# Keeping four weight splits and two gated chunks on chip, moving the residual's loads to GpSimd's queue, and issuing short convolutions behind the next copies

## The chip, the core and the metric

The kernel runs on one core of one Trainium2 chip. The metric is the device time of one execution, in microseconds (us); the time before is the median of three runs. The engines go by the profile's names: PE is TensorE (matmuls), DVE is VectorE, ACT is ScalarE, POOL is GpSimd, SP is SyncE, which here does nothing but issue transfers. POOL and ACT issue transfers too, in the order of their own instructions.

## What is computed

One block of a streaming encoder on a sequence of 1024 tokens with 1024 channels, all in float32:

```python
h = rms_norm(x, norm_mix_g) * (1 + sc1) + sh1
b_s, c_s, v_s, v_c, gl_c, gate_br = split(h @ w_in)          # 7 x 1024 columns
y_a = (b_s * causal_dwconv(c_s * v_s, width 3)) @ w_short_out
u = causal_dwconv(v_c * sigmoid(gl_c), width 31) + conv_conf_b
y_b = silu(layer_norm(u)) @ w_conf_out
g_a, g_b = split(sigmoid(gate_br))
x = x + g1 * ((g_a * y_a + g_b * y_b) @ w_o)
h2 = rms_norm(x, norm_ffn_g) * (1 + sc2) + sh2
a, bgate = split(h2 @ w_ffn_in)                              # 2 x 2816 columns
x = x + g2 * ((silu(a) * bgate) @ w_ffn_out)
return rms_norm(x, final_norm_g)
```

The six vectors sh1, sc1, g1, sh2, sc2, g2 are the modulation, silu(c) @ w_ada + b_ada.

## The kernel before

**Layout and arithmetic.** Channels lie on the 128 partitions, in eight chunks, and the 1024 tokens on the free axis, in two halves of 512. A float32 product is made of three matmuls: each operand is split into a high part (a cast by ACT) and a low part (a subtraction by DVE or POOL), and `mm3` (L315) adds wh·xh, wh·xl and wl·xh (its lines L323, L324 and L326) into one bank of PSUM. Nearly every matmul is 128x128 by 128x512.

**Duals.** Most projections are done two column chunks at a time with seven products in place of eight ("dual"): sums and differences of blocks of the weights, and of blocks of the activations, are multiplied in the order `PRODUCTS = "1265734"`, and each product adds into one of three pairs of banks, x (1, 6, 7, 4), y (2) or z (5, 3). After product "1" ACT copies x to y, and "2" goes on adding there.

**Order of the work.** The kernel is written in the Tile language, which sets the semaphores and decides each engine's order of instructions when it compiles, by the order of the text and by when it reckons things ready. `tc.issue_after(ins)` puts the instructions of a block behind `ins` in the order of the same engine; it makes nobody wait. Weights come from a `plan`: `next_w` (L287) hands out the next unit and sees that the two that follow are begun. A plain unit (`weights`, L211) is a load on SP's queue into one of the raw buffers, a cast (L220) into one of three wh buffers and a subtraction (L221) into one of three wl buffers. Most activations and their splits live in one pool, `t`, of 58 tiles of 128x512.

The stages, with the lines that the change and the prediction's steps touch:

1. *Input projection.* Seven column chunks by plain products, then 14 duals (`win_dual`, L713; dual 0 to 5 have products "1" and "2" done ahead, so their loop begins with "6"). `PAIRS` (L76) says what each dual makes: "u" a channel chunk of the conformer, "p" one of the short convolution, "q" the multiplier of two short-conv chunks, "g" gates. The banks rotate by one pair from dual to dual, so the x banks of one dual are the z banks of the next. At the end of a dual, each "p" has its width-3 convolution done by `short_conv` (L667), which uses the x banks of its dual as room: one ACT activation (L671) and two DVE taps (L674) for each half. Meanwhile DVE does the width-31 convolution, tap by tap (L821), between the evictions. The copy from x to y is L769.
2. *Short-conv projection* `ya`, four column chunks at a time in two duals (L926).
3. *Conformer projection* `yb` (L994), for each half of the tokens in turn: eight weights w_conf[k], eight banks, three matmuls for each pair; the last two weights are done together at the end. The plan lists the eight weights twice, once for each half (L284). `next_b` (L898) makes the operands: a product with the layer norm's scale, silu, split (zs). The banks are evicted by DVE with the gate (L1002) and joined with y_a (L990, then the split into mg).
4. *Output projection* `mix` (L1013). The new residual x1 goes to DRAM (x1_dram), by POOL's queue.
5. *FFN in* (L1105 on): 11 duals, each a pair of gated chunks. `hid_set` (L1168) makes what the next stage multiplies. For the first nine pairs these are seven blocks for seven products; the last two pairs (chunks 18, 19 and 20, 21) are kept as they are, four halves each. `store` (L1161) splits each block into a stage buffer (three of them, 128x1024; ACT L363, DVE L364) and POOL's queue stores it to DRAM (L1166).
6. *FFN out* (L1268 on): three groups of three pairs, in each two duals ("column duals": chunks 0 to 3 with 4 to 7, here called dual 0 and 1 of the group), products of 18 matmuls each. `group_load` (L1197) loads a group's 42 tiles back from DRAM by POOL's queue (L1192) into pool t, the first group during the last dual of stage 5, each next one after the first product of the group before. `out_evac` (L1258) adds each bank onto x1 in place (DVE L1263): products "1", "2", "6" and "3" onto chunks 0 and 1 (dual 1: 2 and 3), "5", "7" and "4" onto 4 and 5 (dual 1: 6 and 7).
7. *Last chunks* 18 to 21 and the final norm, in three pieces of tokens (`piece_out`, L1305).

x1 comes back from DRAM before stage 6: chunks 0 and 1 by POOL's queue (L1251), into a pool of their own; the other six by SP's queue (L1256), in the order 4, 5, 2, 3, 6, 7, into a pool `x1b` that lies where stage 5's pools `gi` (the gated chunks) and `stage` lay.

Of the kernel before, what the change touches and what calls it, by code (L numbers as in the profile page):

```python
# [39 lines left out]
P = 128  # L40
D = 1024
T = 1024
H = 512
KC = D // P
# [55 lines left out]


FRONT = 3


GROUP, GROUPS = 3, 3
# [10 lines left out]
def block_kernel(ctx: ExitStack, tc: tile.TileContext, xt, x0, xT, c, vecs, ada, w_first, w_duals,  # L116
# [164 lines left out]
    ya_units = [dual_units([w_short[d, m] for m in range(4)], 1024, True, lo={"1": nc.vector if d else nc.gpsimd})  # L281
                for d in range(2)]
    plan += [ya_units[d][m] for d, m in ya_order]
    plan += [(w[k], 1024) for w in (w_conf, w_o) for _ in range(2) for k in range(KC)]  # L284
    ready = []

    def next_w(ahead=AHEAD):  # L287
# [141 lines left out]
    x = {}  # L429
# [268 lines left out]
    def q_operands(m):  # L698

        for k in range(KH):  # L700
# [9 lines left out]
                nc.vector.tensor_tensor(b12, b22, b12, ALU.subtract)  # L710
            tq[m][k] = split({"1": b11, "2": b21, "5": b11, "7": b12, "3": b22, "4": b21}[m], hl_tile, "tq")

    def win_dual(d, pairs, x, y, z):  # L713

        mul = any(kind == "q" for kind, *_ in pairs)

        def c11(p, e, kind, j, *more):
            if kind == "q":
                times(sc[j][:, halves[0]], y[p], sc[j][:, halves[0]])
                return  # L720
            first_out(d, p, y[p])

        def c22(p, e, kind, j, *more):
            src = y[p] if kind == "q" else e["5"]
            add = nc.vector.tensor_tensor(src, x[p], e["5"], ALU.add)
            if kind == "q":
                return minus_times(sc[j + 1][:, halves[1]], src, sc[j + 1][:, halves[1]])
            e["z"] = src
            if kind == "g":
                gate_out(more[0], 1, src, src, -1.0)  # L730
            elif kind == "u":
                nc.scalar.activation(src, src, AF.Sigmoid, scale=-1.0)
            return add

        def c12(p, e, kind, j, *more):
            add = nc.vector.tensor_tensor(z[p], z[p], e["6"], ALU.add)
            if kind == "q":
                return times(sc[j][:, halves[1]], z[p], sc[j][:, halves[1]])
            if kind == "u":
                return times(e["b"][1], z[p], e["z"])  # L740
            if kind == "p":
                return minus_times(e["b"][1], z[p], e["z"])
            gate_out(j, 1, z[p], e["6"])
            return add

        def c21(p, e, kind, j, *more):
            if kind == "q":
                return minus_times(sc[j + 1][:, halves[0]], x[p], sc[j + 1][:, halves[0]])
            if kind == "p":
                return minus_times(e["b"][0], x[p], e["b"][0])  # L750
            if kind == "u":
                nc.scalar.activation(x[p], x[p], AF.Sigmoid, scale=-1.0)
                return times(e["b"][0], x[p], e["b"][0])
            gate_out(more[0], 0, x[p], g_tile("sig"), -1.0)

        banks = {"1": x, "6": x, "7": x, "4": x, "2": y, "5": z, "3": z}
        at = 5 * d - 2 if d < AHEAD_DUALS else 7 * d - 2 * AHEAD_DUALS
        if d < AHEAD_DUALS:
            for p in range(2):
                nc.scalar.copy(x[p], m1[d, p])  # L760
        for m in PRODUCTS[2 if d < AHEAD_DUALS else 0 :]:
            w = next_w()
            for p in range(2):
                ps, e = banks[m][p], st[d][p]
                for k in range(KH):
                    c0 = (p * KH + k) * P
                    mm3([ps], slice(c0, c0 + P), w, [th[m][k]], m in "15" and k == 0, k == KH - 1, m not in "15")
                if m == "1":
                    nc.scalar.copy(y[p], ps)  # L769
                elif m in "65":  # L770
                    e[m] = g_tile("v")
                    nc.scalar.copy(e[m], ps)
                else:
                    done = {"2": c11, "7": c22, "3": c12, "4": c21}[m](p, e, *pairs[p])
                    if done is not None:
                        reads.append((at + AT_READS[m] + 0.5 * p, done.ins))
            if m == "6" and d < AHEAD_DUALS - 1:
                m1_load(d + 1)
            if m == "5" and MOD_FROM <= d < MOD_FROM + MOD_DUALS:
                modulation(16 + d - MOD_FROM, uc_tile("ada", D))  # L780
            if d == len(PAIRS) // 2 - 1:
                if m == "1":
                    for j in range(KH):
                        q_load(j)
                if m in "16734":
                    q_operands({"1": "1", "6": "2", "7": "6", "3": "5", "4": "7"}[m])
        for e, (kind, j, *more) in zip(st[d], pairs):
            if kind == "p":
                short_conv(j, e["t"], x)
            elif kind == "q" and j < KH:  # L790
                for i in range(2):
                    q_store(j + i)
# [363 lines left out]
                ha[f, "4"] = t  # L1156
        return evac

    hid_dram = {}

    def store(key, src):  # L1161

        s = stagep.tile([P, T], F32R, tag="stage", name="stage")
        t_split(src, s[:, :H], s[:, H:])
        hid_dram[key] = dram.tile([P, T], F32R, name="hid" + "_".join(map(str, key)))
        nc.gpsimd.dma_start(hid_dram[key], s)  # L1166

    def hid_set(d):  # L1168

        (b11, b12), (b21, b22) = ((ha[2 * d + p, "4"], ha[2 * d + p, "6"]) for p in range(2))  # L1170
        if 2 * d >= REST:
            for p, half in enumerate(((b11, b12), (b21, b22))):
                for h in range(2):
                    store((2 * d + p, h), half[h])
            return
        store((d, "1"), b11)
        store((d, "2"), b21)
        t2 = gip.tile([P, H], F32, tag="g", name="t2")
        nc.vector.tensor_tensor(b11, b11, b12, ALU.subtract)
        minus(t2, b11, b22)  # L1180
        store((d, "6"), t2)
        store((d, "5"), b11)
        nc.vector.tensor_tensor(b12, b22, b12, ALU.subtract)
        store((d, "7"), b12)
        store((d, "3"), b22)
        minus(b21, t2, b21)
        store((d, "4"), b21)
# [64 lines left out]
    close(*phase_2)  # L1252
    x1bp = open_pool("x1b", 6, stack=ctx)[1]
    x1 += [x1bp.tile([P, T], F32, tag="x1", name=f"x1{j}") for j in range(2, KC)]
    for j in (4, 5, 2, 3, 6, 7):
        nc.sync.dma_start(x1[j], x1_dram[j])  # L1256

    def out_evac(d):  # L1258
        def evac(p, m, ps):
# [5 lines left out]
            )  # L1265
        return evac

    hid = {}  # L1268
    n = 2 * GROUP * P
    for g in range(GROUPS):  # L1270
        for d in range(2):
# [2 lines left out]
    for g in range(GROUPS):  # L1274
        for d in range(2):
            banks = {}
            for m in PRODUCTS:
                product(banks, m, to[g, m], out_evac(d))
                if d == 0 and m == "1":
                    if g < GROUPS - 1:  # L1280
                        for q in PRODUCTS:
                            group_load(g + 1, q)
                    else:
                        for h in range(2):
                            for f in range(REST, FC):
                                hid[f, h] = t_load((f, h))


# [164 lines left out]
```

## Time and profile before

| | |
|---|---|
| median of three runs | 1468.57 us (1468.46 to 1469.9) |
| the profiled execution: its own time, its span | 1469.82 us, 1468.0 us |
| PE busy | 1447.8 us, 6393 matmuls |
| DVE busy | 1167.9 us, 1604 instructions |
| ACT busy | 652.7 us, 959 instructions |
| POOL busy | 527.4 us, 466 instructions |
| bytes read from and written to DRAM | 198.90 MB, 62.91 MB |
| mean granted TensorE clock | 0.996 |

The span is the time from the first instruction to the last of one execution that the hardware profiler recorded; that execution's own time is a little longer. A row of the timeline has its start in us from the span's start, its duration, engine, line, operation, the tiles (out<-in), the shapes, and in brackets how long the engine stood idle ahead of it and what ended that. A row of the waits has who waited for whom, then the total in us, how many times, and the longest. A row of the chain of waits has its start, how long, and what. A row of the windows has the stretch, its length, the busy time and (x) count of PE, PE's weight loads, DVE, ACT and POOL, the granted clock, the DMA engines' busy share and GB/s. Matmuls overlap: each shows about 0.39 us, and the next one starts before it ends.

### The profile page before, as it was taken

To read this page: it belongs to the slowest core of one execution; us is meant where nothing else is said; L and a number is where in the kernel's file an instruction comes from. 1 tells how busy PE (TensorE), PEld (TensorE's weight loads), DVE (VectorE), ACT (ScalarE), POOL (GpSimd) and SP (SyncE) were. 2 spreads that over 40 slices of the span, in tenths; PEclk is the share of its full clock that TensorE was granted. 3 is DMA by queue.
4 is the path that set the end of the run, shared out by engine and by line. 5 is a ranking of instruction groups with operands and counts; after the bars stand their busy time and mean duration, and the time that the engine had idled before them with its cause. 6 is when DMAs were issued, how large, how long until landed. Compare 5 with 4: busy or idle time off the path is not lost.

```text
span 1468.0 us, 17816 instructions
## 1 busy us (share of the span) xinstructions
PE 1447.8 (99%) x6393; PEld 1188.4 (81%) x6393; DVE 1167.9 (80%) x1604; ACT 652.7 (44%) x959; POOL 527.4 (36%) x466
## 2 busy tenths in 40 slices
PE   8999999999999999999999999999999999999997
PEld 4778888888888888888888888888888888788887
DVE  6898899999989959999677897677776665676755
ACT  4874443433333446465236565444444443122235
POOL 0028788768777762111022002001011025435105
PEclk9999999999999999999999999999999999999999
DMA  9943554231322346576485348454554459998403
GB/s 380 363 157 117 178 158 129 87 129 59 128 86 73 113 145 220 196 231 204 147 287 187 104 155 274 143 181 167 171 178 148 144 176 375 343 282 269 143 22 115
DMA packets 90618, 262.98 MB, mean 179 GB/s; under 512 B 10401, under 2 KB 12577, under 8 KB 90530
## 3 DMA queue, kind: packets, MB, share of 16 engines
q1 hardware_dynamic: 45952, 149.97, 30.7%
q0 software_dynamic: 37232, 96.49, 20.1%
q10 hardware_dynamic: 7346, 15.40, 2.8%
q8 instruction: 50, 0.82, 0.2%
q14 instruction: 38, 0.31, 0.1%
HBM read 198.90 MB, written 62.91 MB: 178 GB/s over the span
## 4 chain that ended last, share of the span: by engine, by line
PE 51%; issue 4%; DVE 2%; DMA 1%; POOL 1%; ACT 0%; POOLq 0%; DVEq 0%; SPq 0%
PE x L323 8%; PE x L324 8%; PE x L326 8%; PE z L323 4%; PE z L326 4%; PE z L324 4%; PE y L323 3%; PE y L326 3%; PE y L324 3%; PE mix L323 2%; PE mix L326 2%; PE mix L324 2%; PE yb L323 1%; PE yb L324 1%; PE yb L326 1%
## 5 line engine op out<-in xcount | busy, mean ns | idle before, releaser
L220 ACT CAST wh<-raw 128x1024 fp32r<-128x1024 f32 (+3 forms) x262 | 264.6, 1011 | 412.2 <-PE x L324 117.1
L221 DVE TENSOR_TENSOR wl<-raw,wh 128x1024 fp32r<-128x1024 f32 (+2 forms) x180 | 208.5, 1160 | 75.6 <-ACT wh L220 74.2
L221 POOL TENSOR_TENSOR wl<-raw,wh 128x1024 fp32r<-128x1024 f32 x82 | 202.0, 2469 | 90.2 <-ACT wh L220 90.2
L821 DVE SCALAR_TENSOR_TENSOR c<-diff,vec,c 128x512 f32<-128x512 f32 x248 | 179.0, 750 | 2.7
L1166 POOL DMA_DIRECT2D hid<-stage x71 | 37.8, 533 | 336.8 <-DVE stage L364 333.9
L324 PE MATMUL x<-tl,wh 128*128 128x512 f32 x304 | 118.6, 390 | 0.6 <-DVE tl L364 0.6
L323 PE MATMUL x<-th,wh 128*128 128x512 f32 x304 | 118.5, 390 | 0.0
L326 PE MATMUL x<-th,wl 128*128 128x512 f32 x304 | 118.3, 389 | 0.0
L323 PE MATMUL z<-th,wh 128*128 128x512 f32 x216 | 84.6, 392 | 2.1 <-DVE x L1263 2.1
L821 DVE SCALAR_TENSOR_TENSOR c<-u,wsum,c 128x512 f32<-128x512 f32 x112 | 84.1, 751 | 2.0
L326 PE MATMUL z<-th,wl 128*128 128x512 f32 x216 | 84.5, 391 | 0.0
L324 PE MATMUL z<-tl,wh 128*128 128x512 f32 x216 | 84.5, 391 | 0.0
L326 PE MATMUL y<-th,wl 128*128 128x512 f32 x180 | 70.1, 390 | 0.2 <-POOL wl L221 0.2
L324 PE MATMUL y<-tl,wh 128*128 128x512 f32 x180 | 70.0, 389 | 0.0
L323 PE MATMUL y<-th,wh 128*128 128x512 f32 x180 | 70.0, 389 | 0.0
L364 DVE TENSOR_TENSOR stage<-g,stage 128x512 fp32r<-128x512 f32 x62 | 41.9, 688 | 34.5 <-ACT stage L363 34.5
L243 POOL TENSOR_TENSOR raw<-raw 128x1024 f32<-128x1024 f32 x13 | 33.6, 2582 | 95.3 <-DVE t2l L364 78.9
L324 PEld LDWEIGHTS x<-tl,wh 128*128 128x128 f32 x304 | 57.2, 188 | 12.9 <-DVE tl L364 1.0
L323 PEld LDWEIGHTS x<-th,wh 128*128 128x128 f32 x304 | 57.2, 188 | 12.0
L326 PEld LDWEIGHTS x<-th,wl 128*128 128x128 f32 x304 | 57.2, 188 | 11.8
L1192 POOL DMA_DIRECT2D th<-hid x71 | 38.2, 538 | 75.2 <-PE x L326 56.6
L363 ACT CAST stage<-g 128x512 fp32r<-128x512 f32 x62 | 37.4, 619 | 51.8 <-DMA hid<-stage 43.5
(759 smaller groups left out, 4023.4 us busy)
## 6 DMA issues: line engine op xcount, KB each, us to landing
hid<-stage POOLq DMA_DIRECT2D x71, 512.0 KB, 5.2
raw<-in_w_duals SPq DMA_DIRECT2D x66, 512.0 KB, 3.6
raw<-in_w_fi SPq DMA_DIRECT2D x53, 512.0 KB, 4.6
th<-hid POOLq DMA_DIRECT2D x71, 256.0 KB, 5.7
tl<-hid POOLq DMA_DIRECT2D x71, 256.0 KB, 5.8
ada<-in_ada SPq DMA_DIRECT2D x33, 512.0 KB, 6.0
raw<-in_w_fo SPq DMA_DIRECT2D x24, 384.0 KB, 6.5
raw<-in_w_conf SPq DMA_DIRECT2D x16, 512.0 KB, 4.3
```

Of the source, the lines that this page charges most:

```text
L220: hi = nc.scalar.copy(wh, raw)
L221: lo = lo_engine.tensor_tensor(wl, raw, f32(wh), ALU.subtract)
L243: eng.tensor_tensor(a["s1"], a["21"], a["22"], ALU.add)
L323: nc.tensor.matmul(ps, wh, xh, start=first, stop=False, skip_group_check=again)
L324: nc.tensor.matmul(ps, wh, xl, start=False, stop=False, skip_group_check=again)
L326: mm3.ins = nc.tensor.matmul(ps, wl, xh, start=False, stop=last, skip_group_check=again).ins
L363: nc.scalar.copy(hi, src)
L364: t_split.ins = nc.vector.tensor_tensor(lo, src, f32(hi), ALU.subtract).ins
L821: tap.ins = nc.vector.scalar_tensor_tensor(out=out, in0=src[:, s : s + H], scalar=wt, in1=acc, op0=ALU.mult, op1=ALU.add).ins
L1166: nc.gpsimd.dma_start(hid_dram[key], s)
L1192: nc.gpsimd.dma_start(t, hid_dram[key][:, s])
```

## The change

Four things are changed.

- **Kept splits.** Of the eight conformer weights, 2, 3, 4 and 5 (`KEPT`) are loaded and split once, for the first half of the tokens, into tiles of pool t (two halves, high and low: four tiles for a weight, by `split`, lines L354 to L356), and the second half of the tokens uses the same tiles. `Halves` lets a matmul take its 128 columns from the right one.
- **Short convolutions.** For duals 5 to 12 the `short_conv` of a "p" is put off: it is issued in the next dual, after product "1", with ACT's part behind the copies from x to y.
- **Last gated chunks.** The last pair, chunks 20 and 21, is split into tiles of pool t and stays there up to the end; it isn't stored to DRAM and loaded again. Chunks 18 and 19 go on as before.
- **Residual.** Chunks 4 and 5 of x1 are loaded by POOL's queue in place of SP's, and chunks 2, 3, 6 and 7 by POOL's queue as well, in the text after the first product of group 0.

```diff
+KEPT = (2, 3, 4, 5)
...
-    plan += [(w[k], 1024) for w in (w_conf, w_o) for _ in range(2) for k in range(KC)]
+    kept = {}
+
+    class Halves:
+        def __init__(self, tiles):
+            self.tiles = tiles
+
+        def __getitem__(self, at):
+            cut = at[1]
+            return self.tiles[cut.start // H][:, cut.start % H : cut.start % H + P]
+
+    def conf_unit(k, h):
+
+        if k not in KEPT:
+            return weights(w_conf[k])
+        if h == 0:
+            raw = load(w_conf[k])
+            pairs = [split(raw[:, s], hl_tile, "kw") for s in halves]
+            kept[k] = tuple(Halves(t) for t in zip(*pairs))
+            made[id(kept[k][1])] = split.act, split.ins
+        return kept[k]
+
+    plan += [lambda k=k, h=h: conf_unit(k, h) for h in range(2) for k in range(KC)]
+    plan += [(w_o[k], 1024) for _ in range(2) for k in range(KC)]
...
+    y_copies, pending = [], []
+    n_duals = len(PAIRS) // 2
+
+    def run_convs():
+        while pending:
+            with tc.issue_after(y_copies[-1]):
+                short_conv(*pending.pop(0))
+
     def win_dual(d, pairs, x, y, z):
...
                 if m == "1":
-                    nc.scalar.copy(y[p], ps)
+                    y_copies.append(nc.scalar.copy(y[p], ps).ins)
...
+            if m == "1":
+                run_convs()
+        if d < AHEAD_DUALS - 1 or d >= n_duals - 1:
+            y_copies.clear()
         for e, (kind, j, *more) in zip(st[d], pairs):
             if kind == "p":
-                short_conv(j, e["t"], x)
+                if AHEAD_DUALS - 1 <= d < n_duals - 1:
+                    pending.append((j, e["t"], x))
+                else:
+                    short_conv(j, e["t"], x)
...
-    hid_dram = {}
+    hid_dram, hid = {}, {}
...
         if 2 * d >= REST:
             for p, half in enumerate(((b11, b12), (b21, b22))):
                 for h in range(2):
-                    store((2 * d + p, h), half[h])
+                    if d < N_IN - 1:
+                        store((2 * d + p, h), half[h])
+                    else:
+                        hid[2 * d + p, h] = t_pair("hid")
+                        t_split(half[h], *hid[2 * d + p, h])
             return
...
-    for j in (4, 5, 2, 3, 6, 7):
-        nc.sync.dma_start(x1[j], x1_dram[j])
+
+    def x1_load(js):
+        for j in js:
+            nc.gpsimd.dma_start(x1[j], x1_dram[j])
+
+    x1_load((4, 5))
...
-    hid = {}
     n = 2 * GROUP * P
...
                 product(banks, m, to[g, m], out_evac(d))
+                if (g, d, m) == (0, 0, "1"):
+                    with tc.issue_after(mm3.ins):
+                        x1_load((2, 3, 6, 7))
                 if d == 0 and m == "1":
...
                         for h in range(2):
-                            for f in range(REST, FC):
+                            for f in range(REST, FC - 2):
                                 hid[f, h] = t_load((f, h))
```

## The prediction

> **What bounds the kernel now.** I read the page's first table, then TensorE's list of waits, then, at each wait that lies near an edit, the timeline of the engines around it, and last the chain of waits. The profiled execution took 1469.82 us with a span of 1468.0 us; that is 1.25 us over the median of the runs, 1468.57. I work out a difference from the trace and take it off the median.
>
> ```profile
> PE 1447.8 (99%) x6393; PEld 1188.4 (81%) x6393; DVE 1167.9 (80%) x1604; ACT 652.7 (44%) x959; POOL 527.4 (36%) x466
> ...
> PE z L323 <- DVE x L1263: 2.1, 1, 2.1
> ...
> PE z L323 <- DVE ma L683: 0.7, 1, 0.7
> ...
> PE y L323 <- ACT y L769: 0.5, 1, 0.5
> PE yb L323 <- DVE gb L1002: 0.2, 1, 0.2
> ```
>
> TensorE is busy for 99% of the span, so only its few stalls can be won, and a new stall is the only thing that can be lost. The change takes no matmul away. Three rows of the list touch lines of the diff: z behind L1263 (the residual in the last stage), y behind L769 (the copy ahead of which a short conv stands) and yb behind L1002 (the conformer projection, whose splits are kept). The rows give idle time; what a stall costs is the lost distance between starts of matmuls, which I take from the timeline. Its undisturbed value stands between the first and the last of the 24 matmuls of one product:
>
> ```profile
> 254.36 0.39 PE L323 MATMUL x<-h00h,wh 128*128 128x512 f32 x1
> ...
> 259.57 0.39 PE L326 MATMUL x<-h30h,wl 128*128 128x512 f32 x1
> 260.41 0.50 PE L323 MATMUL y<-h40h,wh 128*128 128x512 f32 x1 [0.45 <-ACT y L769]
> ...
> 265.98 0.39 PE L323 MATMUL x<-t2h,wh 128*128 128x512 f32 x1
> ```
>
> 259.57 less 254.36 is 5.21 us for 23 steps, 0.2265 us each. The step into product "2" of dual 6 takes 0.84 us, 0.61 too much, and the 24 steps from there to 265.98 take 5.57 instead of 5.44, 0.13 too much. **The short-conv stall costs 0.74 us.**
>
> ```profile
> 1256.13 0.39 PE L323 MATMUL z<-th,wh 128*128 128x512 f32 x1
> ...
> 1257.95 0.39 PE L326 MATMUL z<-th,wl 128*128 128x512 f32 x1
> 1260.47 0.50 PE L323 MATMUL z<-th,wh 128*128 128x512 f32 x1 [2.13 <-DVE x L1263]
> ...
> 1261.67 0.63 PE L324 MATMUL z<-tl,wh 128*128 128x512 f32 x1
> 1262.10 0.63 PE L326 MATMUL z<-th,wl 128*128 128x512 f32 x1
> ...
> 1272.44 0.39 PE L323 MATMUL y<-th,wh 128*128 128x512 f32 x1
> 1260.00:1268.00 8.00, 7.53 (x26) 6.03 (x27) 4.87 (x7) 0.83 (x1) 0.53 (x1) 0.79 1.11 395
> ```
>
> From 1256.13 to 1272.44 TensorE does three products of 18 matmuls (products "3" and "4" of the first column dual, "1" of the second): 54 steps, 12.23 us undisturbed, 16.31 measured. **The residual's stall costs 4.08 us**, in two pieces: the 2.1 us of waiting, and then some nine matmuls 0.43 us apart (1261.67, 1262.10), in the only stretch here whose granted clock is below 1 (0.79 from 1260 to 1268).
>
> ```profile
> 688.37 0.39 PE L326 MATMUL yb<-zsh,wl 128*128 128x512 f32 x1
> 688.99 0.50 PE L323 MATMUL yb<-zsh,wh 128*128 128x512 f32 x1 [0.23 <-DVE gb L1002]
> ```
>
> Here a step takes 0.62 us: **the conformer stall costs 0.39 us.** All three together are 5.2 us.
>
> **The change part by part.** *Residual and last gated chunks.* SyncE's waits, the engines' timelines and the chain of waits tell why x1 is late:
>
> ```profile
> SPq L1256 <- DMA hid<-stage: 8.2, 1, 8.2
> ...
> 1247.12 0.53 POOL L1166 DMA_DIRECT2D hid<-stage  x1 [5.45 <-DVE stage L364]
> ...
> 1253.29 6.25 DMA x<-x_dram
> ...
> 1259.66 0.76 DVE x L1263
> ...
> 1238.88 0.69 DVE L364 TENSOR_TENSOR stage<-g,stage 128x512 fp32r<-128x512 f32 x1
> ...
> 1252.94 0.96 DVE L221 TENSOR_TENSOR wl<-raw,wh 128x768 fp32r<-128x768 f32 x1
> ```
>
> The fourth store of the last gated pair waits for a free stage buffer (there are three), so GpSimd's queue stands for 5.45 us and the store goes out at 1247.12; x1[5] overlays a stage buffer and waits 8.2 us for that store to land; its load lands 6.25 us after 1253.29, and the update at 1259.66 reads it. TensorE needs that bank again for product "3", second half, which would start at 1257.95 + 0.23 = 1258.18. The change takes the four stores out: the last pair is split into tiles of pool t. Then no stage buffer is waited for, and the gi tiles under x1[4] and x1[5] are read for the last time by some 1240 (the third subtraction ends at 1238.88 + 0.69, and one more of 0.69 follows). Four casts and four subtractions stay as they are. GpSimd's queue loses four issues of 0.53 us here and, with the eight loads less at the last group, eight more; it gains six for x1, 3.2 us, and group 1's loads stand behind them, which are first read after six more products of 18 x 0.2265 = 4.08 us, at 1272.44 + 24.5 = 1296.9. SyncE's queue loses the 8.2 us in which the w_fo loads behind x1 were held.
>
> How long x1[4] and x1[5] take on GpSimd's queue this trace shows only at another load and another hour. I bound it by
>
> ```profile
> DMA to landing us min/median/max: 7.5/7.9/8.2
> DMA to landing us min/median/max: 6.2/9.0/13.5
> ```
>
> x1[0] and x1[1] over GpSimd's queue (L1251) and the six over SyncE's (L1256), these in the same busy stretch (DMA share 1.11). From 1240 that lands between 1246.2 and 1253.5. I take 9.0, the median of the same transfers in the same stretch, 1249. x1[5]'s update (0.75 us) must begin by 1257.4, so at either end 3.9 us or more are left. The stall goes with all of its 4.08 us; what comes next, the weights of product "4", is there from 1252.94 + 0.96 on, six us before it is read. If that cover were gone, up to 4.08 us would stay. In the last group 42 tiles of to[2], eight of hid 20 and 21, and eight of 18 and 19 are the same 58 tiles of pool t as before; in group 1 eight fewer can be loaded ahead, and what is left has a whole half group, 28 us, to come in. I cost that at nothing.
>
> By the Trainium skill ("SBUF — State Buffer", section "SBUF: two separate sides") a load issued from GpSimd can be held up by VectorE, since GpSimd's software writes its descriptors through a port pair that it shares with VectorE, and the page advises SyncE's or ScalarE's queue; by that rule rival (3) below would be the likely case, and the sum -1.1 us in place of -5.2. The two rows above speak against it: the GpSimd loads are no slower.
>
> *Short convs behind the next copies.* ScalarE's rows at the late copy:
>
> ```profile
> 259.19 0.69 ACT L671 ACTIVATE z<-p,vec 128x512 f32<-128x512 f32 x1
> 259.82 0.54 ACT L769 COPY y<-x 128x512 f32<-128x512 f32 x1
> ```
>
> The second activation of the short conv (0.63 from start to start) stands right ahead of the copy. Without it the copy begins at 259.19 or before and ends by 259.73; TensorE wants it at 259.57 + 0.23 = 259.80. The 0.74 us go, or 0.1 of it stays. Nothing is removed, though: two activations and four taps for each of six short convs run 6 to 9 us later, and their bank is the z bank of the next dual, which product "5" writes. Worst is dual 11, which has two:
>
> ```profile
> 481.79 0.69 ACT L671 ACTIVATE z<-p,vec 128x512 f32<-128x512 f32 x1 [2.58 <-DVE p L683]
> ...
> 490.01 0.58 ACT L769 COPY y<-x 128x512 f32<-128x512 f32 x1
> ...
> 489.05 0.75 DVE L674 SCALAR_TENSOR_TENSOR z<-p,vec,z 128x512 f32<-128x512 f32 x1
> ...
> 490.36 0.74 DVE L674 SCALAR_TENSOR_TENSOR sc<-p,vec,z 128x512 f32<-128x512 f32 x1
> ...
> 499.90 0.39 PE L323 MATMUL z<-th,wh 128*128 128x512 f32 x1
> 460.00:500.00 40.00, 40.00 (x178) 33.13 (x177) 39.30 (x56) 14.37 (x20) 29.88 (x14) 1.00 0.30 93
> ```
>
> The two took from 481.79 to 491.10, 9.3 us, some of it waiting for their inputs, which will be there by then. Begun at 490.6 they end at 499.9 at this pace; TensorE needs the first bank at 499.90 and the second 2.7 us later. The last two taps stand 1.31 apart with one conformer tap between, so a place is 0.66; back to back (0.69 and eight places) they would be done at 496.6. So the cost lies between 0 and some 0.7 us; I take 0, as the first bank's last tap is not the last one. VectorE is full there (39.30 of 40 us), so order is all that changes.
>
> *Kept splits.* Of the second half's eight conformer weights four are neither loaded nor cast nor subtracted. At the stall VectorE runs two such subtractions just ahead of the eviction that TensorE waits for:
>
> ```profile
> 685.98 2.35 DVE L221 TENSOR_TENSOR wl<-raw,wh 128x1024 fp32r<-128x1024 f32 x2
> 688.25 0.68 DVE L1002 TENSOR_TENSOR gb<-yb,gb 128x512 f32<-128x512 f32 x1
> ...
> 640.52 0.69 DVE L683 SCALAR_TENSOR_TENSOR ma<-y,ma 128x512 f32<-128x512 f32 x1 [0.93 <-PE y L326]
> ...
> 643.46 0.68 DVE L356 TENSOR_TENSOR zsl<-cv,zsh 128x512 fp32r<-128x512 f32 x1
> 645.76 0.39 PE L323 MATMUL yb<-zsh,wh 128*128 128x512 f32 x1
> ```
>
> They are the weights 1 and 2 of the second half; 2 is kept, so one of 1.17 us goes, the eviction ends near 687.8 and TensorE's 688.60 is met: 0.4 us gone. In the first half each kept weight is subtracted in two pieces of 0.68 (the row of that shape) against 1.17, so 0.2 more each at most. They need no wh or wl buffer and can run earlier: then they push the second operand's split, done at 643.46 + 0.68 for matmuls that start at 645.76. That is 1.6 us of room, against two kept weights (2.4 us) put ahead at most: 0 to 0.8 us. I take 0, since VectorE stood idle (0.93 us) just before, where they fit.
>
> **Sum:** -4.08 - 0.74 - 0.39 = -5.2 us, 1468.57 to 1463.4, a span of 1462.8.
>
> **The rivals.** (1) *Small stalls move, the large one goes*: one of the two bounds above comes true (0.7, 0.8 us) and one of the two small gains fails. Then 1463.4 + 1.4 = 1464.8. For it speaks VectorE's 39.30 of 40 us; against it, that the list of waits has no z behind taps (L674) and no yb behind zsl. (2) *The slow clock stays*: only waiting goes, and the stretch at 0.43 us apart (nine times 0.2, 1.8 us) comes anyway, at another place: 1465.2. The granted clock below 1 right behind the only 2 us stall in mid kernel speaks against it. The Trainium skill ("TensorE: Matmul & The Clock Gate", Part 1) has the clock halve after about 3.4 us without work, and by that rule a 2.13 us wait would not have done it; the trace disagrees. (3) *The residual is late all the same*, or the second part is not held back (the block that should hold it names a TensorE instruction, while the loads are GpSimd's, so I count on the order of the text alone): if the queue stands for another wait until 1248, as it did before, and the loads then take the longest time seen, they land at 1261.5 and the 4.08 us stay: 1467.5, no measurable difference. (4) *Slower*: the deferred short convs of dual 11 hold TensorE at 499.90. VectorE works in a fixed order; if conformer taps take two places of three, eight short taps need 24 x 0.66 = 15.8 us, end at 491.3 + 15.8 = 507.1, and TensorE waits 7.2 us and then loses about 1.8 us more at the low clock: 1463.4 + 9.0 = 1472.4. It stalls from a last tap at 499.9 on; at 503.3 wait and slow clock (3.4 + 1.8) have eaten the gain. In the trace a short tap has one conformer tap between it and the next (489.05 to 490.36), which speaks against it.
>
> **How the numbers follow.** Forecast 0.70, rival (1) 0.13, (2) 0.03, (3) 0.08, (4) 0.06. About 0.2% (2.9 us) is what a measurement of this kernel can tell from no change: below 1465.6 counts as faster. Forecast, (1) and (2) are faster, 0.86; (3) is within, 0.08; (4) slower, 0.06. The range takes in the forecast, (1) and (2) with half a us for the runs' scatter, up to 1465.8; downward the z wait of 0.7 us behind L683, which a new order may also clear, and the same half give 1462.2.
>
> **What would show it.** Right: z no longer waits for L1263, the granted clock stays 1.00 from 1250 to 1300, x1[4] and x1[5] are issued near 1240 and land before 1255; y does not wait for L769; yb does not wait for L1002 near 684; TensorE's waits hold no new entry above 0.5 us. Wrong: a wait of z for short-conv taps (L674) near 500, of yb for zsl or wl near 646, or a GpSimd queue that stands before x1.

## The result, and the profile after

The changed kernel takes 1465.74 us (median of ten runs, 1463.85 to 1466.44) against 1469.32 for the kernel before (ten runs, the three of the table above among them, 1468.07 to 1472.89). The ratio is 0.9967, with a 95% interval of 0.9959 to 0.9976: 3.5 to 6.0 us faster. (This ratio and those below are estimated over the runs and are not quotients of the two medians, which would be 0.9976 here.) The profiled execution took 1464.61 us and has a span of 1462.8 us, against 1468.0: 5.2 us shorter. HBM reads fall from 198.90 to 194.70 MB and writes from 62.91 to 60.82 MB.

Lines up to 101 keep their place; further down those of the changed kernel are shifted. `mm3` is L348, L349 and L351, the weights' cast and subtraction L223 and L224, the activations of a short conv L696 and its taps L699, the copy to y L802, the residual's update L1311, its six late loads L1302, the conformer's eviction L1042.

The page's first line after, and TensorE's whole list of waits after (who waited for whom: us in total, times, longest):

```profile
PE 1445.3 (99%) x6393; PEld 1187.2 (81%) x6393; DVE 1157.1 (79%) x1604; ACT 647.9 (44%) x959; POOL 521.3 (36%) x460
```

```profile
PE rx L481 <- ACT spread L473: 2.7, 1, 2.7
PE lead L510 <- POOL idle L503: 1.7, 1, 1.7
PE lead L348 <- ACT m L581: 1.5, 1, 1.5
PE x L348 <- ACT x L793: 1.3, 1, 1.3
PE x L349 <- DVE tl L389: 0.6, 1, 0.6
PE y L351 <- POOL wl L224: 0.6, 1, 0.6
PE z L348 <- DVE ma L708: 0.2, 1, 0.2
```

All three waits that the change was costed by are gone, and no new one stands in their place. The matmuls are as many as before. The stretch that held the slow clock before (0.79), in the view by stretches, is at 1.00, with TensorE busy throughout:

```profile
1260.00:1268.00 8.00, 8.00 (x37) 6.63 (x36) 6.00 (x9) 1.67 (x2) 1.99 (x4) 1.00 0.08 22
```

**The residual.** TensorE's timeline after, product "3" of the first column dual, the first matmul of each half, and the first of product "4"; then, of the same stretch, GpSimd's issues for x1 and VectorE's updates of chunks 4 and 5:

```profile
1254.88 0.39 PE L348 MATMUL z<-th,wh 128*128 128x512 f32 x1
...
1256.92 0.39 PE L348 MATMUL z<-th,wh 128*128 128x512 f32 x1
...
1258.96 0.39 PE L348 MATMUL x<-th,wh 128*128 128x512 f32 x1
```

```profile
1238.61 2.28 POOL L1302 DMA_DIRECT2D x<-x_dram  x4 [0.16 <-issue]
1241.25 1.20 POOL L1302 DMA_DIRECT2D x<-x_dram  x2 [0.36 <-DVE wl L224]
...
1248.96 0.75 DVE L1311 SCALAR_TENSOR_TENSOR x<-z,ng,x 128x512 f32<-128x512 f32 x1 [0.39 <-PE z L351]
...
1251.01 0.75 DVE L1311 SCALAR_TENSOR_TENSOR x<-z,ng,x 128x512 f32<-128x512 f32 x1 [1.29 <-PE z L351]
```

Nothing stands between the halves: 18 steps from 1254.88 to 1258.96 take 4.08 us, which is 18 x 0.2265. The loads are issued near 1240, as worked out; the first two, chunks 4 and 5, land 5.9 and 6.6 us later, and the updates wait for TensorE's product and no longer for a load. The "two parts" of the residual's loads can't be told apart: all six issues stand between 1238.6 and 1242.5. The last z update ends at 1251.8, some 5 us before the bank is used again.

**The short convs.** ScalarE's copy and TensorE's step into product "2" of dual 6; then dual 12's ScalarE and VectorE rows, in which the two convs of dual 11 run, and TensorE's first use of their bank:

```profile
259.51 0.58 ACT L802 COPY y<-x 128x512 f32<-128x512 f32 x1
...
259.91 0.39 PE L351 MATMUL x<-h30h,wl 128*128 128x512 f32 x1
...
260.14 0.50 PE L348 MATMUL y<-h40h,wh 128*128 128x512 f32 x1
260.48 0.39 PE L349 MATMUL y<-h40l,wh 128*128 128x512 f32 x1
```

```profile
490.25 1.29 ACT L696 ACTIVATE z<-p,vec 128x512 f32<-128x512 f32 x2
...
490.97 1.41 DVE L699 SCALAR_TENSOR_TENSOR z<-p,vec,z 128x512 f32<-128x512 f32 x2 [0.65 <-ACT z L696]
...
495.52 1.40 DVE L699 SCALAR_TENSOR_TENSOR sc<-p,vec,z 128x512 f32<-128x512 f32 x2
...
496.84 5.36 DVE L861 SCALAR_TENSOR_TENSOR c<-diff,vec,c 128x512 f32<-128x512 f32 x8
...
499.64 0.39 PE L348 MATMUL z<-th,wh 128*128 128x512 f32 x1
```

Of 0.74 us at the copy 0.11 are left (a step of 0.34 in place of 0.23). The eight taps stand nearly back to back and the last ends at 496.92, 2.7 us before TensorE wants the first bank; the conformer taps were put behind them.

**The kept splits.** VectorE's and TensorE's rows at the conformer's eviction: one subtraction of 1.22 us stands ahead of the eviction, where two (2.35) stood, and the next matmul follows after 0.23 us.

```profile
685.85 1.22 DVE L224 TENSOR_TENSOR wl<-raw,wh 128x1024 fp32r<-128x1024 f32 x1
...
686.99 0.68 DVE L1042 TENSOR_TENSOR gb<-yb,gb 128x512 f32<-128x512 f32 x1
...
687.57 0.39 PE L351 MATMUL yb<-zsh,wl 128*128 128x512 f32 x1
687.80 0.43 PE L348 MATMUL yb<-zsh,wh 128*128 128x512 f32 x1
```

**Where the time went.** Adding up, over the whole trace, what each distance of more than 0.28 us between starts of matmuls has above 0.228 gives 30.7 us before and 25.3 after. Of the 5.4 us, 3.96 are at the residual, 0.61 at the copy and 0.50 at the conformer's eviction. The rest nearly cancels: the step behind L708 at 615 us costs 0.54 less, the one behind GpSimd's subtraction at 221 us 0.33 more.

### The profile page after: what moved, and what is told of

Same layout as the page of the kernel before. It is cut to its first block, busy times and chain, and to the rows that moved or that the text cites. A ratio compares the mean times of both kernels' runs of the same rounds, so it can differ in the third digit from the quotient of the medians.

```text
span 1462.8 us, 17754 instructions
## 1 busy us (share of the span) xinstructions
PE 1445.3 (99%) x6393; PEld 1187.2 (81%) x6393; DVE 1157.1 (79%) x1604; ACT 647.9 (44%) x959; POOL 521.3 (36%) x460
## 3 DMA queue, kind: packets, MB, share of 16 engines
HBM read 194.70 MB, written 60.82 MB: 175 GB/s over the span
## 4 chain that ended last, share of the span: by engine, by line
PE 79%; DVE 4%; issue 1%; POOL 1%; DMA 1%; POOLq 0%; ACT 0%; DVEq 0%
PE x L348 10%; PE x L351 10%; PE x L349 10%; PE z L348 7%; PE z L349 7%; PE z L351 7%; PE y L351 6%; PE y L348 6%; PE y L349 6%; PE yb L351 2%; PE mix L351 2%; PE mix L349 2%; PE yb L349 2%; PE yb L348 2%; PE mix L348 2%
## 5 line engine op out<-in xcount | busy, mean ns | idle before, releaser
L223 ACT CAST wh<-raw 128x1024 fp32r<-128x1024 f32 (+3 forms) x254 | 256.1, 1009 | 401.0 <-PE x L349 138.0
L224 DVE TENSOR_TENSOR wl<-raw,wh 128x1024 fp32r<-128x1024 f32 (+2 forms) x172 | 198.9, 1157 | 69.4 <-ACT wh L223 68.3
L224 POOL TENSOR_TENSOR wl<-raw,wh 128x1024 fp32r<-128x1024 f32 x82 | 201.3, 2460 | 91.6 <-ACT wh L223 91.4
L349 PE MATMUL x<-tl,wh 128*128 128x512 f32 x304 | 118.4, 389 | 0.6 <-DVE tl L389 0.6
L351 PE MATMUL x<-th,wl 128*128 128x512 f32 x304 | 118.3, 389 | 0.0
L348 PE MATMUL x<-th,wh 128*128 128x512 f32 x304 | 118.3, 389 | 0.0
L348 PE MATMUL z<-th,wh 128*128 128x512 f32 x216 | 84.0, 389 | 0.0
L349 PE MATMUL z<-tl,wh 128*128 128x512 f32 x216 | 84.0, 389 | 0.0
L351 PE MATMUL z<-th,wl 128*128 128x512 f32 x216 | 84.0, 389 | 0.0
L351 PE MATMUL y<-th,wl 128*128 128x512 f32 x180 | 70.1, 390 | 0.6 <-POOL wl L224 0.6
L348 PE MATMUL y<-th,wh 128*128 128x512 f32 x180 | 70.0, 389 | 0.0
L349 PE MATMUL y<-tl,wh 128*128 128x512 f32 x180 | 70.0, 389 | 0.0
L246 POOL TENSOR_TENSOR raw<-raw 128x1024 f32<-128x1024 f32 x13 | 33.1, 2548 | 96.4 <-DVE t2l L389 79.0
L349 PEld LDWEIGHTS x<-tl,wh 128*128 128x128 f32 x304 | 57.1, 188 | 12.8 <-DVE tl L389 1.0
L351 PEld LDWEIGHTS x<-th,wl 128*128 128x128 f32 x304 | 57.1, 188 | 11.9
L348 PEld LDWEIGHTS x<-th,wh 128*128 128x128 f32 x304 | 57.1, 188 | 11.9
L329 DVE CUSTOM_DVE_ANT_0 ada<-ada,cs,vec 128x1024 f32<-128x1024 f32 x33 | 46.0, 1410 | 13.2 <-DMA ada<-in_ada 12.1
```

What stands on the lines that cost most here:

```text
L223: hi = nc.scalar.copy(wh, raw)
L224: lo = lo_engine.tensor_tensor(wl, raw, f32(wh), ALU.subtract)
L246: eng.tensor_tensor(a["s1"], a["21"], a["22"], ALU.add)
L329: modulation.ins = nc.vector.tensor_tensor_reduce(out=raw, in0=raw, in1=cs, scale=1.0, scalar=col(V_ADA, b), op0=ALU.mult, op1=ALU.add, ac ...
L348: nc.tensor.matmul(ps, wh, xh, start=first, stop=False, skip_group_check=again)
L349: nc.tensor.matmul(ps, wh, xl, start=False, stop=False, skip_group_check=again)
```

## The experiments

All edits are shown against the changed kernel. Each was timed against the kernel before on one chip; medians of different groups aren't compared. First each part by itself.

### The residual's part alone

```diff
-KEPT = (2, 3, 4, 5)
+KEPT = ()
...
-                if AHEAD_DUALS - 1 <= d < n_duals - 1:
+                if False:
```

> Only the last gated pair on chip and the residual's loads on GpSimd's queue; no kept splits, short convs at their old place. The prediction's step: the 4.08 us stall of z behind L1263 goes, the stalls of 0.74 (y behind the copy) and 0.39 us (yb behind the eviction) stay: span 1468.0 - 4.1 = 1463.9, ratio 0.9972. Rival, the gain comes from less DMA traffic and less VectorE work spread over the kernel: less than 2 us from this part alone, ratio over 0.9986.

Measured: 1465.84 us against 1470.33, 0.9971 [0.996, 0.9982]. No wait is left near 1258, and the clock is 1.00 from 1255 to 1268; the wait of y for the copy (0.5 us of waiting, 0.72 of lost distance) is still there. So this part carries nearly all of the gain, and the rival (over 0.9986) lies outside its interval. The profiled execution's span is 1466.1, since it lost 1.7 us to a slow stretch at 42 us and 1.8 at 221, where no part of the change is.

### The short convs alone, and the kept splits alone

The first edit leaves only the deferral, the second (all hunks of the first but that of `KEPT`, and the deferral switched off as above) only the kept splits.

```diff
-KEPT = (2, 3, 4, 5)
+KEPT = ()
...
-                    if d < N_IN - 1:
+                    if True:
...
-            nc.gpsimd.dma_start(x1[j], x1_dram[j])
+            nc.sync.dma_start(x1[j], x1_dram[j])
...
-    x1_load((4, 5))
+    x1_load((4, 5, 2, 3, 6, 7))
...
-                if (g, d, m) == (0, 0, "1"):
-                    with tc.issue_after(mm3.ins):
-                        x1_load((2, 3, 6, 7))
...
-                            for f in range(REST, FC - 2):
+                            for f in range(REST, FC):
```

> Only the short convs behind the next copies. The prediction's step: y no longer waits for the copy, -0.74 us, span 1467.3, ratio 0.9995, which the interval may not part from 1. Rival (4): TensorE waits for the z bank behind the taps in dual 12, a new wait of z for L674's taps near 500 us, 1 us or more slower.

> Only the four kept splits. The prediction's step: yb no longer waits for its eviction near 688 us, -0.39 us, span 1467.6, ratio 0.9997. Rival: in the first half the earlier subtractions push the operands' split, a new wait of yb for zsl near 646 us, up to 0.8 us lost.

Measured: 1470.45, 0.9995 [0.9983, 1.0008], and 1469.99, 0.9994 [0.9982, 1.0006]: neither can be told from no change by its time, as the sizes (0.7 and 0.4 us of 1470) would have it. The traces tell more. With the deferral alone the wait of y is gone and no wait for taps appears near 500; with the kept splits alone no yb wait near 690 and none for zsl near 646. (The second has a wait of 0.7 us for a weight's subtraction at 574 us that the changed kernel doesn't have; why is open.) In both the residual's stall is back. TensorE's timeline of the first, then of the second:

```profile
1260.13 0.39 PE L351 MATMUL z<-th,wl 128*128 128x512 f32 x1
1263.26 0.59 PE L348 MATMUL z<-th,wh 128*128 128x512 f32 x1 [2.74 <-DVE x L1311]
1263.65 0.63 PE L349 MATMUL z<-tl,wh 128*128 128x512 f32 x1
1264.08 0.63 PE L351 MATMUL z<-th,wl 128*128 128x512 f32 x1
```

```profile
1257.51 0.39 PE L351 MATMUL x<-th,wl 128*128 128x512 f32 x1
1261.65 0.47 PE L348 MATMUL z<-th,wh 128*128 128x512 f32 x1 [3.75 <-issue]
```

The distance over the wait is 3.13 and 4.14 us, where it was 2.52 before, and each is followed by a stretch at 0.43 us a matmul (1263.65 to 1264.08 in the first), which costs 1.7. So the residual's stall costs 4.1 to 5.6 us in these three traces, and 4.08 was its small end.

The conformer's stall is less firm than my 0.39 says. In the four other traces without kept splits the two subtractions also stand together ahead of the eviction, and TensorE loses 0.4 us there (short convs alone), 0.2 (residual alone) or nothing (both runs of the next section). The kept splits take away the cause; what they save is 0 to 0.5 us, by execution.

### Which half of the residual's part: the chip or the queue

The first kernel keeps the last pair on chip, but loads x1 by SyncE's queue in the old order. The second stores the pair as before, and loads x1 by GpSimd's queue. Both without the other two parts.

```diff
-            nc.gpsimd.dma_start(x1[j], x1_dram[j])
+            nc.sync.dma_start(x1[j], x1_dram[j])
...
-    x1_load((4, 5))
+    x1_load((4, 5, 2, 3, 6, 7))
...
-                if (g, d, m) == (0, 0, "1"):
-                    with tc.issue_after(mm3.ins):
-                        x1_load((2, 3, 6, 7))
```

> Last gated pair on chip, but the residual's six loads on SyncE's queue in their old order; no kept splits, short convs at their old place. If the cause was the last store through the stage buffer (my step), x1[5] needs no more wait and the stall goes without the other queue: span 1463.9, ratio 0.9972, the same as with GpSimd's queue. If the queue is what cures it (rival), the stall stays: span 1468.0, ratio 1.000.

Measured: 1466.74 against 1470.33, 0.9973 [0.9962, 0.9983], span 1463.3, no stall at the residual. SyncE's six issues before and in this run, and this run's row of the windows at the residual:

```profile
1243.23 12.38 SPq L1256 DMA_DIRECT2D x<-x_dram  x6
```

```profile
1242.08 3.54 SPq L1302 DMA_DIRECT2D x<-x_dram  x6
...
1255.00:1268.00 13.00, 13.00 (x59) 10.77 (x58) 9.44 (x13) 2.78 (x4) 1.43 (x3) 1.00 0.27 101
```

The six issues, which the wait of 8.2 us for the store had spread over 12.4 us, now stand within 3.5, and TensorE is busy throughout. The store through the stage buffer was the cause; with the queue moved as well the same comparison gave 0.9971, so that move adds nothing that can be measured.

```diff
-                    if d < N_IN - 1:
+                    if True:
...
-                            for f in range(REST, FC - 2):
+                            for f in range(REST, FC):
```

> The residual's loads on GpSimd's queue in two parts, but the last gated pair still stored to DRAM and loaded again; no kept splits, short convs at their old place. My theory: x1[5] still waits for the fourth store to land (near 1253 us), now inside GpSimd's queue, so the stall of z stays at 4.1 us or is longer by up to 1: span 1468.0 to 1469.0, ratio 1.000 to 1.0007. Rival (the queue is the cure): span 1463.9, ratio 0.9972.

Measured: 1467.36 against 1470.85, 0.9981 [0.9971, 0.9991], span 1465.4. Its interval lies 1.3 to 4.3 us below the kernel before: the theory's number isn't in it, and the rival's only at its edge. GpSimd's and VectorE's rows of its timeline, and below them TensorE's:

```profile
1247.16 0.53 POOL L1206 DMA_DIRECT2D hid<-stage  x1 [5.16 <-DVE stage L389]
...
1249.25 0.57 POOL L1302 DMA_DIRECT2D x<-x_dram  x1
...
1252.45 2.08 POOL L1302 DMA_DIRECT2D x<-x_dram  x4 [2.64 <-DMA hid<-stage]
...
1256.39 0.75 DVE L1311 SCALAR_TENSOR_TENSOR x<-z,ng,x 128x512 f32<-128x512 f32 x1 [5.81 <-PE x L351]
...
1258.79 0.74 DVE L1311 SCALAR_TENSOR_TENSOR x<-z,ng,x 128x512 f32<-128x512 f32 x1
```

```profile
1255.90 0.39 PE L351 MATMUL x<-th,wl 128*128 128x512 f32 x1
1257.24 0.47 PE L348 MATMUL z<-th,wh 128*128 128x512 f32 x1 [0.95 <-ACT wh L223]
```

The mechanism is as I had it: the fourth store goes out at 1247.16, at the same time as before, and the queue stands for it (2.64 us until it has landed). But its size is not what I expected: chunks 4 and 5 then land just ahead of their updates at 1256.39 and 1258.79 (landing took 6.0 to 9.7 us), and TensorE waits in two small pieces, 1.1 and 0.2 us, with the clock at 1.00 throughout: 1.5 us in all, 2.6 less than 4.08. (That its span is shorter by 2.6 too is partly chance: this trace also loses 1.1 us between 480 and 520 us and wins 0.5 at the conformer's eviction. The profile puts the 0.95 down to a cast; the bank that the matmul writes was freed by the update that ended at 1257.14, so it is the residual.) x1[5] lands at 1258.48 here and at 1259.54 before, 1.1 us earlier, and the stall that is left has no slow clock behind it. That part of the 4.08 us is not proportional.

### What a wait costs, by itself

Ten, then thirteen, VectorE operations that multiply the last z bank by 1 are put ahead of its update, with the order of the products held by hand, so that TensorE waits at the place of the old stall (the lines that hold the order are left out here):

```diff
+            n_out[0] += 1
+            if n_out[0] == 8:
+                for _ in range(10):
+                    nc.vector.tensor_scalar(ps, ps, 1.0, None, ALU.mult)
```

> The changed kernel with a made-up short wait at the old place: ten extra VectorE instructions (each multiplies the bank of product 5, second half, by 1 in place) ahead of the bank's addition to x1[5], and the products after it kept in that order. At 0.60 to 0.70 us each the bank comes free 0.9 to 1.9 us after TensorE wants it for product 3. My theory now (half of the residual's 4.08 us was the low clock, which only waits of about 2.1 us and more have brought on in these runs): the wait alone is lost, no stretch of low clock, span 1462.8 + 0.9 to 1.9. Rival (the low clock follows any wait in proportion): about twice that.

> The same with thirteen extra instructions: a wait of 2.7 to 4.0 us, 1.8 to 2.1 us more than with ten. Theory: one stretch of low clock, 3.4 us long, follows, which costs 1.7 us beside the wait: 3.5 to 3.8 us slower than with ten, span 1467.2 to 1468.5. Rival (a wait shorter than 3.4 us leaves the clock alone): 1.8 to 2.1 us slower than with ten.

Measured: 1467.75, 0.9986 [0.9977, 0.9995], and 1471.77, 1.0008 [0.9999, 1.0016], both against 1471.0. TensorE's timeline of the ten, then of the thirteen:

```profile
1257.49 0.39 PE L351 MATMUL z<-th,wl 128*128 128x512 f32 x1
1259.94 0.50 PE L348 MATMUL z<-th,wh 128*128 128x512 f32 x1 [2.06 <-DVE x L1317]
1260.28 0.40 PE L349 MATMUL z<-tl,wh 128*128 128x512 f32 x1
```

```profile
1256.56 0.39 PE L351 MATMUL z<-th,wl 128*128 128x512 f32 x1
1261.20 0.50 PE L348 MATMUL z<-th,wh 128*128 128x512 f32 x1 [4.26 <-DVE x L1317]
...
1261.80 0.63 PE L351 MATMUL z<-th,wl 128*128 128x512 f32 x1
1262.23 0.63 PE L348 MATMUL z<-th,wh 128*128 128x512 f32 x1
```

Both waits came out longer than I had put them, and so did the spans, 1466.0 and 1468.9. The first costs its own 2.3 us and no clock; the second 4.4 us, and then 3.4 us at half the clock, which cost 1.7 more. The medians differ by 4.0; in the traces the losses at this place differ by 3.8, the spans by 2.9. So the long stall cost its wait and a further sum, which the short one did not have. As the thirteen's wait is itself over 3.4 us, this pair doesn't decide between a limit there and a lower one; the rows of the other runs do (last section).

### How much room the short convs have

Each deferred short conv is done twice, to the same values (the loop inside `short_conv` is left out here):

```diff
-                short_conv(*pending.pop(0))
+                short_conv(*pending.pop(0), 2)
```

> The changed kernel with each deferred short conv done twice over (the same activations and taps a second time, the same values), to find out how much room there is ahead of the z bank. In the changed kernel dual 11's two convs end at 496.9 us and TensorE writes the bank at 499.6. Twice the work would end near 503.6, the first bank's last tap some 0.7 us before: TensorE waits about 3.3 us for z behind the taps in dual 12 and, as after the 2.1 us wait of before, loses up to 1.8 us more at the low clock; span 1462.8 + 3 to 5 = 1466 to 1468. The other deferred duals, with one conv each, end 7 us after the copy with 10 us of room: no wait. Rival: the convs give way to conformer taps or are not what the bank waits for: no wait of z, span within 0.5 us of 1462.8.

Measured: 1477.01 (six runs), 1.0058 [1.0041, 1.0075], span 1474.8, some 12 us above the changed kernel. ScalarE's rows and TensorE's at the end of dual 12's first products:

```profile
502.97 0.69 ACT L697 ACTIVATE z<-p,vec 128x512 f32<-128x512 f32 x1 [0.53 <-DVE sc L700]
503.60 0.58 ACT L806 COPY v<-x 128x512 f32<-128x512 f32 x1
```

```profile
500.36 0.39 PE L351 MATMUL x<-t2h,wl 128*128 128x512 f32 x1
504.23 0.50 PE L348 MATMUL x<-th,wh 128*128 128x512 f32 x1 [3.48 <-ACT v L806]
...
572.30 0.50 PE L351 MATMUL z<-tqh,wl 128*128 128x512 f32 x1 [3.30 <-POOL wl L224]
```

So rival (4)'s direction is real, but its path is another. The bank that holds TensorE is an x bank. The engines' order is made when the kernel is compiled, and with twice the work TensorE takes a product into x ahead of "5"; ScalarE's copy out of that bank stands in its queue behind the activations of the repeated convs, which wait for VectorE. A second stall of 3.3 us follows where the conv stage ends late, and each has a half-clock stretch of 3.4 us behind it. The two places lose 5.4 and 6.0 us; the 3 to 5 expected count only one such place, and put it a little low. One round of convs fits, two don't.

### Two tries to go further

One of the small waits that are left, y for GpSimd's subtraction at 221 us, is taken off by giving one subtraction to VectorE; and the front's wait at 38 us by asking for one prepared operand less there:

```diff
-                              {m: nc.vector for m in "12"}, d == 0) for d in range(AHEAD_DUALS)]
+                              {m: nc.vector for m in ("124" if d == 4 else "12")}, d == 0) for d in range(AHEAD_DUALS)]
```

> The changed kernel with one low part (product 4 of the fifth front dual) subtracted by VectorE in place of GpSimd, whose 2.4 us subtraction is the wait of 0.6 us (y for wl near 221 us) that the changed kernel still has; it costs 0.82 us there. VectorE's takes 1.2 us: the wait goes, span 1462.0, 0.8 us under the changed kernel. Rival: VectorE, full there, comes later with it or with an eviction behind it: the same or slower than the changed kernel.

```diff
-        while len(ops) < min(k + 1 + BEFORE, KC):
+        while len(ops) < min(k + 1 + BEFORE - (k == KH - 1), KC):
```

> A version that should beat the changed kernel: it with the sixth input chunk's operands made one step later in the text (BEFORE counts one less at the fourth chunk), so that ScalarE's copies of the half-way sums (m, L581) are not queued behind a cast that waits for VectorE. The changed kernel loses 1.85 - 0.23 us there and 0.45 right after (TensorE's wait lead behind m, near 38 us), and in some executions 1.7 us of low clock behind it. If the order is the cause: the wait goes, span 1462.8 - 2.0 = 1460.8, ratio to the kernel before 0.995. Rival: the sixth chunk's operands then come late themselves, a new wait of lead for h50 or wh near 43 us, span 1462.8 or more.

Measured: 1470.03 against 1470.85, 0.9998 [0.9987, 1.0009], and 1466.43 against 1471.0, 0.9968 [0.9957, 0.998]. In each the wait aimed at is gone and a larger one has come up elsewhere. TensorE's row of the first, far behind the edit, and of the second:

```profile
619.15 0.53 PE L348 MATMUL z<-tqh,wh 128*128 128x512 f32 x1 [2.55 <-DVE ma L708]
```

```profile
90.24 0.50 PE L348 MATMUL x<-t2h,wh 128*128 128x512 f32 x1 [2.36 <-ACT x L793]
```

In the first VectorE's order from 595 us on came out otherwise: two preparations of weights (L246 and L247, 1.2 us each), which the changed kernel does before the evictions at L991, come behind them, and the z eviction begins at 618.32 in place of 615.10. Between 600 and 640 us that and a slow stretch cost 5.6 us more than in the changed kernel. In the second a wait of 1.9 us, for the operand h70h, has come at 52 us, and the one at 90 us, 1.3 in the changed kernel, is 2.36 with a slow stretch behind it. The changed kernel run once more beside the first,

> The changed kernel again, on the chip of the other runs of this call, to compare them with it: span 1462.8, ratio 0.9965 by the trace's difference of 5.2 us (0.9967 was measured).

gave 1465.23, 0.9972 [0.996, 0.9984], span 1462.9. Against it the first, 1470.03 on the same chip, is slower, and the second's 0.9968 lies within its interval: neither beats it.

## Why the prediction was right, and where its reasons were off

- **Sum and span.** 1468.0 less 5.2 is 1462.8, and that is the span. The trace's three terms, 4.08, 0.74 and 0.39, came out as 3.96, 0.61 and 0.50 by the count above. That the span agrees to the tenth is partly luck: the profiled execution before lies 0.5 us above the median of its ten, the one after 1.1 below. The medians show 3.6, which the sums of rivals (1) and (2), 3.8 and 3.4, would meet as well, and 1465.74 is at the upper end of the range, 2.3 over the forecast. The interval of 3.5 to 6.0 holds the 5.2; it is the traces, and the parts run alone, that speak for the forecast's reasons. Executions differ by as much at places where the change has no edit: a slow stretch near 40 us (1.7 us) is in three of the thirteen traces, the changed kernel's second one among them, and the wait at 221 us costs 0 to 1.8.
- **The residual's stall** went with all of its 4.08, for the reason given: the store that waited for a stage buffer. The run with the pair on chip and SyncE's queue shows it. The same run shows that the queue's change was not needed, which the forecast had left open by pricing the two together. The landing of x1[4] and x1[5] by GpSimd's queue, taken at 9.0 us each, was 5.9 and 6.6, at the short end of the bounds; 8.9 is the median of all six.
- **Where it was off: the 4.08 as one term.** The prediction named its two pieces, but in rival (3), "the 4.08 us stay", took them to go or stay together. It is 2.3 us of lost distance at the wait and 1.8 behind it, nearly all at the half clock, and the shorter wait put in at the same place had no second piece. With stores kept and the queue moved, 1.5 us stayed of it, and the rest went.
- **Rival (2), the slow clock comes anyway:** refuted by the traces. After, no granted clock below 1 is recorded between 16 and 1458 us; the kernel's second trace has a slow stretch at 40 us, but behind a wait of its own there (2.27 us from start to start). In the pair of added waits the half clock follows the long stall.
- **Rival (1)'s two unknowns**, the deferral (0 to 0.7) and the order of the kept splits (0 to 0.8), both came out at 0 beside their gains, and 0.11 us of the copy's stall was left, as the text allowed.
- **Rival (4)**, the deferred convs: eight places back to back, the 496.6 that the prediction worked out, and 496.92 in the trace. The times at which it would stall were worked out for the z bank alone; done twice, the convs hold TensorE through ScalarE's queue first.
- **The kept splits:** right in the trace, but the stall of 0.39 us that they remove isn't in every execution.

## What to carry to other kernels

Where TensorE is busy for 99%, the busy share says nothing more: add up what each distance between matmul starts has above the undisturbed one, and price an edit by the places where it stands. A load that comes late is best followed back through the buffer that it overlays: here a store, queued behind a stage buffer's release, held a load that nothing else held, and keeping that data on chip freed it whichever queue issued it. And a small wait is worth an edit only if the edit leaves the order of the engines elsewhere alone, since here a single subtraction, moved to another engine to win 0.8 us, cost some 5 us 400 us further on.

## What the runs showed of the hardware

- **A half clock of fixed length behind a long pause.** In all thirteen traces (from 35 us to the last matmul), eight distances of 2.52 us and more between two matmul starts (2.52, 2.75, 2.94, 3.13, 3.69, 3.87, 4.14, 4.65) were each followed, within some 5 us from the pause's start, by one stretch of 3.41 us at half the clock, costing about 1.7 us. None of 1.87 and less was. Of fourteen from 1.9 to 2.45 three were (1.92, 2.06 and 2.27, all at 38 us) and eleven not (2.42 and 2.45 among them), so the length alone doesn't decide there; what does is open. (Those three were 1.5 to 1.9 us idle, so the 2.1 us that the expectation of the ten names is no lower limit.) By the Trainium skill ("TensorE: Matmul & The Clock Gate", Part 1) it takes an idle window of about 3.4 us for the clock to halve. The slow stretch is as long as that (3.41); of the pauses that brought it, those up to 3.13 us from start to start are shorter.
- **GpSimd's queue beside a busy VectorE.** x1's six loads on GpSimd's queue, in the answer for their line, of the changed kernel:

```profile
DMA to landing us min/median/max: 5.9/8.9/12.6
```

In the run with the pair on chip and SyncE's queue the same loads took 8.9, 10.7 and 11.9 us (five of the six are recorded), and before, on SyncE's, 6.2, 9.0 and 13.5. By the Trainium skill ("SBUF — State Buffer", section "SBUF: two separate sides") loads issued by GpSimd are held up while VectorE runs an instruction in a mode that locks GpSimd out of the ports that the two share, as a float32 copy within SBUF does. VectorE is busy for 10.78 of the 14 us from 1238 to 1252 here, and no such delay is seen in these rows. But its instructions there are TENSOR_TENSOR and SCALAR_TENSOR_TENSOR, none a copy, so no run here tests that case.
